# New TensorE prices in the list scheduler of a two-layer mixer and feed-forward kernel

## The chip, the cores and the metric

The kernel runs on one core of one Trainium2 chip. The metric is the device time of one execution in microseconds (us); the median of the runs is the figure to compare, and a profile of one execution says where the time goes.

The core has five engines that run at once, each through its own list of instructions in a fixed order: TensorE (PE in the profile; its weight loads are PEld), VectorE (DVE), ScalarE (ACT), GpSimd (POOL) and SyncE (SP), which here issues the DMA transfers. They wait for each other through semaphores.

## The reference

Two layers work on 256 latent tokens and 256 context tokens of width 1024. Each layer scales and shifts its input by values computed from a conditioning vector, runs four kinds of attention side by side, adds their projections through gates, projects the sum, normalises, and then runs a feed-forward network. The second layer computes the latent tokens alone.

```python
for l in range(DEPTH):                                   # DEPTH = 2
    mod_l = s_lat @ w_ada[l] + b_ada[l]                  # six rows of 1024: shifts, scales, gates
    hl = xl * (1.0 + sc1) + sh1                          # and the same for the context tokens
    out_l, out_c = token_mixers(hl, hc, ...)             # MLA, neighbourhood, differential, grouped-query
    xl = layer_norm(ALPHA * xl + g1 * out_l, ln1_g[l], ln1_b[l])
    hl = xl * (1.0 + sc2) + sh2
    xl = layer_norm(ALPHA * xl + g2 * swiglu(hl, w_gate_up[l], w_down[l]), ln2_g[l], ln2_b[l])
    # context tokens: the same, in the first layer only
```

In each attention, softmax(q k) over up to 512 keys multiplies v; the branch outputs are multiplied by sigmoid gates of the same input projection.

## The kernel before

Every float32 product is made of three matmuls on rounded operands: each operand is split into a high part (rounded to the type fp32r) and the rest, and high x high, high x low and low x high are summed (`mm3`). A weight block of 128 x 1024 is loaded by a DMA (tile `wr`), ScalarE rounds it (`wh`), and VectorE subtracts (`wl`). TensorE then runs over eight slices of 128 input channels with 512 moving columns (256 in the second layer). Softmax runs per head and per 128 queries: scores on TensorE (tile `st`), maximum on VectorE, exponential on ScalarE (tile `P`), scaling, then transposes of `P` on TensorE, a split of the result (`pth`, `ptl`), and the product with v (tile `o`).

The program doesn't emit these instructions as it meets them. `Plan.record` (line 249) notes each operation with the tiles that it reads and writes, and asks `price` (line 280) for its duration. When the whole program has been noted, `schedule` (line 313) orders it. It runs up to ten passes (PASSES, line 227). A pass has two halves:

- `forward` (line 382) plays the program through with the prices. Each engine is free again after the price of what it last ran. Among the operations of an engine that can start by then, the one of least priority number goes first. An operation can start when its predecessors have ended, plus an allowance for the signal between the two engines (SEE, lines 220 to 223), and when its tile has a buffer.
- `backward` (line 333) plays it from the end and gives each operation its priority for the next pass: how long before the end it has to run.

The pass whose modelled end is earliest is kept. `emit` (line 514) then writes the instructions out phase by phase, in the order of their modelled starts, so this sets the order of every engine's queue, the DMA queue of SyncE among them, and which buffer each tile takes. A new phase begins before the attention part of each layer and again before its feed-forward part. No modelled time reaches the chip: there only the order within each queue and the semaphores count.

The prices of the other engines stand in the same function: VectorE's is 0.065 us and one element a cycle at 0.96 GHz, ScalarE's 0.05 or 0.09 us and 0.833 ns an element, and a DMA's goes by its bytes.

All instructions are issued in `emit`, so the profile gives all of them line 535, and they are told apart by the names of their tiles.

Of the kernel before, what the change touches and what calls it, by code (L numbers as in the profile page):

```python
# [11 lines left out]
F32R = mybir.dt.float32r  # L12
# [219 lines left out]
class Plan:  # L232
# [47 lines left out]
    def price(self, op, ins, outs):  # L280

        eng, kw = op.eng, op.kw
        if eng == "tensor":
            if op.meth == "transpose":
                n = kw["in_"].shape[0]
                return max(64, n) * 2.1 / 2400
            n = max(64, kw["rhs"].free())
            return n / 2400 + 0.0026 if kw["rhs"].dtype == F32R else n * 4 / 2400 + 0.43
        n = max([v.free() for v in outs + ins] or [1])
        ps_in = any(v.tile.pool.psum for v in ins)  # L290
        ps = ps_in or any(v.tile.pool.psum for v in outs)
        if eng == "scalar":
            ptr = sum(1 for k in ("bias", "scale") if isinstance(kw.get(k), View)) + ("accum_out" in kw)
            return (0.05 if ps_in else 0.09) + n * 0.833e-3 + 0.093 * ptr
        if eng == "vector":
            if op.meth == "reciprocal":
                return 0.065 + n * 8 / 960
            ptr = sum(1 for k in ("scalar", "scalar1", "scalar2") if isinstance(kw.get(k), View))
            if op.meth == "tensor_scalar" or op.meth == "tensor_copy":
                return 0.065 + 0.06 * ptr + n / 960 / (1 if ps else 2)  # L300
            return 0.065 + 0.065 * ptr + n / 960
        if eng == "gpsimd":
            if kw.get("op") == ALU.pow:
                return 0.3 + n * 0.17
            return 0.16 + n * 2.2e-3
        op_bytes = 1
        for v in (outs or ins):
            op_bytes = v.shape[0] * v.free() * 4
        op.bytes = op_bytes
        op.dge = 0.65 if outs and ins else 0.46  # L310
        return 0.05
# [1513 lines left out]
```

## Time and profile before

| | before |
|---|---|
| median of 3 runs | 1371.51 us (1370.48 to 1372.27) |
| the profiled execution, its own time | 1370.68 us |
| its span, first to last instruction | 1368.9 us |
| TensorE busy | 1349.6 us, 99% |
| VectorE busy | 1007.4 us, 74% |
| ScalarE busy | 658.8 us, 48% |
| moved by DMA | 223.83 MB, 164 GB/s in the mean |

An engine is busy while an instruction of it is shown. Consecutive matmuls overlap in the profile, because each is shown until its modelled end while the next has already begun; the rate of TensorE is therefore read from the distance of two starts, and not from the length of one instruction. The idle time that a row shows before an instruction, and the engine and tile that ended it, come from the semaphores.

### The profile page before, as it was taken

What the parts mean: (1) busy time and instruction counts of PE and PEld (TensorE: products, weight loads), DVE (VectorE), ACT (ScalarE), POOL (GpSimd) and SP (SyncE); (2) the same over time, 40 slices, a digit from 0 to 9 for tenths busy, and PEclk for the clock granted to TensorE, in tenths of its full rate; (3) what the DMA queues carried; (4) which work ended last, traced back from release to release, by engine and by line L of the source; (5) the groups of instructions that cost most, each with busy time, mean ns of one, the idle gap of its engine ahead of it and who ended that gap; (6) DMA issues with size and microseconds to landing.
All of it is one profiled execution on the core that took longest, in us unless ns stands there. A gap on an engine that the chain in (4) does not pass through costs nothing.

```text
span 1368.9 us, 20741 instructions
## 1 busy us (share of the span) xinstructions
PE 1349.6 (99%) x7804; PEld 1176.9 (86%) x7804; DVE 1007.4 (74%) x1786; ACT 658.8 (48%) x1177; POOL 65.2 (5%) x123
## 2 busy tenths in 40 slices
PE   7999999999999999999999999999999999999997
PEld 5789889888878889888888888899999999899986
DVE  6787799997885768777655463768879878855554
ACT  6666576634663413232223112457856575544430
POOL 0000100032000000000000000101000200000000
PEclk9999999999999999999999999999999999999999
DMA  8843434344336614556666664255344457655550
GB/s 313 271 126 113 134 112 130 102 154 151 104 112 214 228 39 147 183 193 193 195 205 197 209 194 148 76 176 162 101 135 149 141 195 270 197 186 185 188 181 31
DMA packets 72820, 223.83 MB, mean 164 GB/s; under 512 B 9697, under 2 KB 13969, under 8 KB 72721
## 3 DMA queue, kind: packets, MB, share of 16 engines
q1 hardware_dynamic: 72720, 222.52, 50.6%
q8 instruction: 61, 1.00, 0.3%
q14 instruction: 39, 0.31, 0.1%
HBM read 212.76 MB, written 1.07 MB: 156 GB/s over the span
## 4 chain that ended last, share of the span: by engine, by line
PE 94%; DVE 2%; POOL 1%; ACT 1%; DMA 1%; issue 1%; POOLq 0%; DVEq 0%; SPq 0%; ACTq 0%
PE mm L535 83%; PE st L535 8%; PE o L535 3%; DMA wr<-in_w_a 0%; POOL rms L535 0%; DVE wl L535 0%; ACT wh L535 0%; DVE x L535 0%; DVE ptl L535 0%; POOL rk L535 0%; DMA wr<-in_w_ada 0%; DVE raw L535 0%; ACT raw L535 0%; POOL lnr L535 0%; ACT pth L535 0%
## 5 line engine op out<-in xcount | busy, mean ns | idle before, releaser
L535 ACT CAST wh<-wr 128x1024 fp32r<-128x1024 f32 (+2 forms) x261 | 265.7, 1024 | 386.4 <-PE mm L535 312.8
L535 PE MATMUL mm<-hh,wh 128*128 128x512 f32 (+1 forms) x1248 | 423.4, 340 | 0.8 <-ACT wh L535 0.7
L535 PE MATMUL mm<-hl,wh 128*128 128x512 f32 (+1 forms) x1246 | 422.8, 339 | 0.0
L535 PE MATMUL mm<-hh,wl 128*128 128x512 f32 (+1 forms) x1248 | 422.2, 339 | 0.0
L535 DVE TENSOR_TENSOR wl<-wr,wh 128x1024 fp32r<-128x1024 f32 (+3 forms) x260 | 308.6, 1191 | 141.9 <-ACT wh L535 138.3
L535 PEld LDWEIGHTS mm<-hh,wh 128*128 128x128 f32 x1248 | 235.8, 189 | 25.9 <-ACT wh L535 1.4
L535 PEld LDWEIGHTS mm<-hh,wl 128*128 128x128 f32 x1248 | 235.6, 189 | 24.4
L535 PEld LDWEIGHTS mm<-hl,wh 128*128 128x128 f32 x1246 | 235.5, 189 | 23.0
L535 DVE CUSTOM_DVE_ANT_0 y<-wr,silbc 128x1024 bf16<-128x1024 f32 x80 | 96.6, 1222 | 48.8 <-DMA wr<-in_w_ada 48.7
L535 PE MATMUL mm<-wl,hh 128*128 128x256 f32 (+3 forms) x344 | 110.4, 321 | 0.0
L535 PE MATMUL mm<-wh,hh 128*128 128x256 f32 (+3 forms) x344 | 110.2, 322 | 0.0
L535 PE MATMUL mm<-wh,hl 128*128 128x256 f32 (+3 forms) x344 | 110.2, 321 | 0.0
L535 PE MATMUL mm<-wl,fh 128*128 128x512 f32 (+1 forms) x270 | 101.6, 376 | 0.0
L535 PE MATMUL mm<-wh,fl 128*128 128x512 f32 (+1 forms) x270 | 101.6, 376 | 0.0
L535 PE MATMUL mm<-wh,fh 128*128 128x512 f32 (+1 forms) x270 | 101.4, 377 | 0.0
L535 DVE TENSOR_REDUCE s<-st 128x1 f32<-128x512 f32 (+1 forms) x120 | 70.7, 597 | 7.9 <-PE st L535 6.3
L535 ACT ACTIVATE P<-st,s 128x512 f32<-128x512 f32 (+1 forms) x96 | 59.0, 617 | 28.3 <-DVE s L535 27.6
L535 PE MATMUL mm<-y,wh 128*128 128x512 f32 (+1 forms) x256 | 68.7, 344 | 0.2 <-ACT wh L535 0.2
L535 PEld LDWEIGHTS mm<-wh,hh 128*128 128x128 f32 x344 | 64.7, 189 | 4.5 <-DVE y L535 0.3
L535 PEld LDWEIGHTS mm<-wh,hl 128*128 128x128 f32 x344 | 64.9, 189 | 4.0
L535 PEld LDWEIGHTS mm<-wl,hh 128*128 128x128 f32 x344 | 64.9, 189 | 3.7
L535 DVE TENSOR_TENSOR ptl<-st,pth 128x512 fp32r<-128x512 f32 (+1 forms) x96 | 56.4, 594 | 7.6 <-ACT pth L535 6.9
(273 smaller groups left out, 2021.3 us busy)
## 6 DMA issues: line engine op xcount, KB each, us to landing
wr<-in_w_ada SPq DMA_DIRECT2D x87, 512.0 KB, 3.7
wr<-in_w_gu SPq DMA_DIRECT2D x80, 512.0 KB, 4.3
wr<-in_wa SPq DMA_DIRECT2D x74, 512.0 KB, 3.7
wr<-in_w_dn SPq DMA_DIRECT2D x44, 512.0 KB, 3.4
wr<-in_w_br SPq DMA_DIRECT2D x16, 512.0 KB, 3.5
wr<-in_w_out SPq DMA_DIRECT2D x16, 512.0 KB, 5.4
wr<-in_w_gq SPq DMA_DIRECT2D x8, 512.0 KB, 3.4
bc<-in_lnrows SPq DMA_DIRECT2D x16, 256.0 KB, 3.3
```

Of the source, the lines that this page charges most:

```text
L535: o.ins = getattr(getattr(nc, o.eng), o.meth)(*args, **kw)
```

## The change

`price` gets new numbers for TensorE, and nothing else is edited. A transpose was priced by its rows at 2.1 cycles each; it now costs 0.108 us, or 0.09 us where its input has at most 32 rows. A matmul was priced by its columns at 2.4 GHz and 0.0026 us more (another formula stood for plain float32 operands); it now costs its columns, at least 256, at 2.4 GHz and 0.0134 us more.

```diff
         if eng == "tensor":
             if op.meth == "transpose":
-                n = kw["in_"].shape[0]
-                return max(64, n) * 2.1 / 2400
-            n = max(64, kw["rhs"].free())
-            return n / 2400 + 0.0026 if kw["rhs"].dtype == F32R else n * 4 / 2400 + 0.43
+                return 0.108 if kw["in_"].shape[0] > 32 else 0.09
+            return max(256, kw["rhs"].free()) / 2400 + 0.0134
```

The instructions, their operands and their phases stay the same. What may differ is their order in each engine's queue within a phase, and the buffer that a tile takes.

## Rows read from the trace of the kernel before

**Rows 1.** The page, part 1: busy us (share of the span) xinstructions, by engine.
```profile
PE 1349.6 (99%) x7804; PEld 1176.9 (86%) x7804; DVE 1007.4 (74%) x1786; ACT 658.8 (48%) x1177; POOL 65.2 (5%) x123
```

**Rows 2.** Busy time by stage: stretch, length, engines' busy us, granted clock, DMA share, GB/s.
```profile
0.00:40.00 40.00, 32.02 (x173) 20.89 (x174) 27.17 (x61) 26.83 (x41) 2.81 (x11) 1.00 0.90 319
...
400.00:410.00 10.00, 8.60 (x40) 6.62 (x39) 6.03 (x9) 6.97 (x9) 0.00 (x0) 1.00 0.05 14
...
515.00:868.00 353.00, 353.00 (x1619) 292.78 (x1618) 219.16 (x317) 90.87 (x116) 1.46 (x4) 1.00 0.57 181
...
1115.00:1125.00 10.00, 9.15 (x69) 8.13 (x68) 7.90 (x13) 5.94 (x9) 0.00 (x0) 1.00 0.26 82
...
1200.00:1360.00 160.00, 160.00 (x1162) 151.60 (x1161) 85.81 (x104) 63.69 (x88) 1.68 (x2) 1.00 0.48 154
1360.00:1369.00 9.00, 0.91 (x8) 0.70 (x6) 4.55 (x9) 0.00 (x0) 1.68 (x2) 0.78 0.31 117
sum 1369.00, PE 1349.62 PEld 1176.90 DVE 1007.38 ACT 658.76 POOL 65.21; mean PE 134.96 PEld 117.69 DVE 100.74 ACT 65.88 POOL 6.52
```

**Rows 3.** What TensorE's matmuls waited for: us in total, times, longest us.
```profile
PE st L535 <- ACT pth L535: 6.0, 1, 6.0
PE mm L535 <- DVE wl L535: 1.4, 1, 1.4
...
PE mm L535 <- ACT wh L535: 0.8, 3, 0.4
PE mm L535 <- ACT raw L535: 0.6, 1, 0.6
...
PE mm L535 <- DVE qr L535: 0.2, 1, 0.2
```

**Rows 4.** TensorE's timeline in three stretches: start us, length us, instruction (merged rows xcount).
```profile
700.18 0.39 PE L535 MATMUL mm<-hl,wh 128*128 128x512 f32 x1
700.41 0.39 PE L535 MATMUL mm<-hh,wl 128*128 128x512 f32 x1
...
1220.14 0.28 PE L535 MATMUL mm<-hh,wh 128*128 128x256 f32 x1
1220.26 0.28 PE L535 MATMUL mm<-hl,wh 128*128 128x256 f32 x1
...
201.62 0.60 PE L535 MATMUL st<-ident,P 128*128 128x128 f32 x4
201.98 0.48 PE L535 MATMUL mm<-hh,wh 128*128 128x512 f32 x1
202.29 0.40 PE L535 MATMUL mm<-hl,wh 128*128 128x512 f32 x1
```

**Rows 5.** TensorE's timeline at the end of the first attention part.
```profile
407.26 0.27 PE L535 MATMUL st<-ident,ada 128*8 128x128 f32 x1
408.94 0.50 PE L535 MATMUL mm<-y,wl 128*128 128x512 f32 x1 [1.40 <-DVE wl L535]
```

**Rows 6.** VectorE's timeline in an attention stage: a weight split and the next instruction.
```profile
229.52 1.23 DVE L535 TENSOR_TENSOR wl<-wr,wh 128x1024 fp32r<-128x1024 f32 x1
230.67 0.21 DVE L535 SCALAR_TENSOR_TENSOR s<-s,lam,dfs 128x1 f32<-128x1 f32 x1
```

**Rows 7.** TensorE's timeline in the second layer: a chain's last score matmul and its transposes.
```profile
970.34 0.39 PE L535 MATMUL st<-k,q 96*128 96x512 f32 x1
...
973.73 0.60 PE L535 MATMUL st<-ident,P 128*128 128x128 f32 x4
```

**Rows 8.** ScalarE's timeline there: the scaling of that chain's probabilities.
```profile
972.73 0.73 ACT L535 ACTIVATE P<-P,s 128x512 f32<-128x512 f32 x1
```

**Rows 9.** Instructions on tile P, whole span: the last step of every chain, by engine.
```profile
L535 ACT ACTIVATE P<-P,s x48: 710/724/739, 78.2 to 1111.5; 128x512 f32<-128x512 f32 x48
L535 DVE TENSOR_SCALAR P<-P,s x24: 332/354/357, 80.6 to 390.4; 128x256 f32<-128x256 f32 x24
L535 DVE SCALAR_TENSOR_TENSOR P<-P,s,P x24: 469/740/753, 225.8 to 1055.2; 128x512 f32<-128x512 f32 x16, 128x256 f32<-128x256 f32 x8
```

## The prediction

> **What bounds the kernel now.** I read the page's busy shares first, then the busy time by stage, then the list of what TensorE waited for, and last TensorE's own timeline. The page says TensorE: it is busy 1349.6 us of a span of 1368.9 us, VectorE 74% of it [rows 1]. The table by stage says where the rest is [rows 2]: its sum row has 1349.62 us busy in 1369.00 us, 19.38 us idle. The first 40 us hold 7.98 us of it and the last 9 us 8.09 us. That leaves 3.31 us for everything between 40 and 1360 us, of which 1.40 us lie at 400 to 410 us and 0.85 us at 1115 to 1125 us, where the attention part of a layer ends and its feed-forward part begins. The two long feed-forward stretches, 515 to 868 us and 1200 to 1360 us, hold none: 513 us in which no order can win idle time back. The list of waits [rows 3] has 6.0 us for the first weights in the head and six waits in the middle, of 1.4, 0.8 (three), 0.6 and 0.2 us. Not one of them is for the probabilities of a softmax chain.
>
> A caution on "busy": a matmul of 512 columns is shown as 0.39 us long while the next one starts 0.23 us behind it [rows 4], so idle time is shown only beyond the 0.16 us by which they overlap. The wait shown as 1.40 us is a gap from 407.26 to 408.94 us behind a transpose that takes 0.11 us: 1.57 us lost [rows 5]. For six such waits I add 6 x 0.16 = 1.0 us, so the stalls in the middle cost about 4.3 us.
>
> **The change part by part.** It changes numbers that only the planner reads. Each engine still gets the same instructions, on the same tiles' shapes, in the same phases; what may move is the order on every one of the five queues inside a phase, the DMA queue of SyncE included, and which buffer a tile gets.
>
> First, are the new prices what the trace shows? Matmuls of 512 columns start at 700.18 and 700.41 us, 0.23 us apart; those of 256 columns at 1220.14 and 1220.26 us, 0.12 us apart [rows 4]. The new price gives 512 / 2400 + 0.0134 = 0.2267 us and 256 / 2400 + 0.0134 = 0.1201 us; the old one gave 0.2159 and 0.1093 us. Four transposes and the matmul behind them take from 201.62 to 202.29 us; 0.67 us less 0.23 us for the matmul leaves 0.11 us for each transpose [rows 4], against 0.108 us new and 0.112 us old. So the new prices are right to about 3% and the old ones were 5% to 9% low on every matmul. The branch for plain float32 operands that goes had no user: every matmul here moves fp32r. It costs nothing.
>
> Second, what does that do to the plan's balance? The program issues 3630 matmuls of 512 columns, 3244 of 256, 198 of 384, 192 of 288 and 540 transposes, 7804 in all, as the page counts them [rows 1]. By the old prices they come to 1253.6 us, by the new ones to 1330.5 us: 7264 matmuls x 10.8 ns = +78.5 us, 524 transposes x -4 ns and 16 small ones x +34 ns = -1.6 us. Against 1349.6 us shown busy, the new sum leaves 19.1 us, or 2.4 ns an instruction, for overlap, small waits and switches between transposes and matmuls. The planner's VectorE prices already are intervals: a weight split of 1024 columns is priced at 0.065 + 1024 / 960 = 1.13 us, and the next instruction starts 1.15 us after it, though it is shown as 1.23 us long [rows 6]. So the old plan let TensorE run 6% too fast beside a VectorE priced rightly, and the new one has both right. TensorE stays the engine with the most work in either plan, so neither has a reason to leave it waiting on purpose.
>
> Third, the terms of the sum, against the profiled execution (span 1368.9 us, its run 1370.68 us, which is 0.83 us under the median of 1371.51 us; I carry the differences over to the median):
> - TensorE's work: 0. No instruction is added or removed. The granted clock is 1.00 in every stage but the last, that is at the 2.4 GHz level, and no gap here is big enough for me to expect a change [rows 2]. The 2.4 ns an instruction depend a little on the order (how often a transpose sits between matmuls); I let them stay and give them 2 us either way.
> - Head: 0. The first 6.0 us wait for the first weight block and its rounding, before any matmul can start [rows 3]; the DMA engines are 0.90 busy for 40 us [rows 2], so no order of matmuls makes the data come sooner. What could move is 7.98 - 6.0 = 2.0 us. If the order there got worse, that would cost about as much.
> - Feed-forward stretches: 0, with no idle time to win, and with VectorE at 219 us of 353 us and 86 us of 160 us as cover [rows 2]. If that cover went, a weight split that came late would cost one of its 1.15 us.
> - Tail: 0. Behind the last matmul runs a chain of VectorE, GpSimd and an output transfer that has no alternative order of consequence; 8.09 us stay.
> - The stalls in the middle, 4.3 us: all redrawn, since the planner tries ten passes, keeps the one whose modelled length is least, and now models another length. No row of before shows what the new order stalls on. Bounds: all gone, -4.3 us; or as many again, +4.3 us. With a truer TensorE the planner sees better when it will run out of matmuls at the two phase ends, so I take -1 us, half of their 2.25 us of shown idle time.
> - The softmax chains: 0 now, see the second rival; bounds 0 and +4.8 us. I take 0, as the tightest chain that I read still has its margin.
>
> Sum: -1 us, 1371.5 - 1.0 = 1370.5 us. What a measurement of this kernel can tell from no change is about 0.2%, 2.7 us, so the likeliest case is "no change".
>
> The Trainium skill speaks against the new prices: "TensorE: Matmul & The Clock Gate", section "Back-to-back issue gap", gives the warm gap of an isolated matmul as columns / 2.4 GHz plus about 2.5 ns, which is nearly the old price and would make TensorE's work here 1253.6 us. The trace disagrees, with 0.23 us for 512 and 0.12 us for 256 columns [rows 4] where that formula gives 0.216 and 0.109 us; by that formula the span would hold some 115 us of idle time, and it shows 19.4 us.
>
> **The rivals.**
> Faster: the old plan's error caused the stalls that are left, and with the right ratio they go. For it: the largest one, 1.40 us, is a wait for a VectorE weight split at a phase end [rows 2, 3], the kind that a planner with a wrong ratio misplaces. Against it: there is little to win. At most 4.3 us in the middle and 2.0 us in the head, 6.3 us; I take two thirds, -4.2 us: 1367.3 us.
>
> Slower: the old error was a safety margin, and the new plan spends it. Where the planner fills the time of a softmax chain with other matmuls, the old prices made it put in 5% to 9% more of them than fit. A chain from 970.34 us, its last score matmul, to 973.73 us, its first transpose, lasts 3.39 us [rows 7]; 4.8% of it (all 512 columns) is 0.16 us, 9% (all 256) 0.30 us. The scaled probabilities were done at 972.73 + 0.73 = 973.46 us [rows 8], so this chain had 0.27 us to spare: less 0.16 to 0.30 us, it sits about at zero, part of which the signal between engines takes. There are 48 + 24 + 24 = 96 such chains [rows 9]. For it: TensorE waits for none of them now [rows 3]. Against it: the planner has its own allowance for the signal between engines, and a chain is late only where nothing else is queued ahead of it. It decides from the point at which about a sixth of the chains (18 x 0.15 us = 2.7 us) come late; if a third do, by 0.15 us each, it is 32 x 0.15 = +4.8 us: 1376.3 us.
>
> The change does not do what it says: TensorE's stretches are so long beside the others' that the order where it matters stays as it is, and the time with it, 1371.5 us. For it: in the feed-forward stretches one engine sets the pace in either plan. Against it: a chain of 3.39 us holds over a dozen matmuls, so the prices move what fits into it by more than one of them. I count it within "no change".
>
> **How the numbers follow.** Forecast, no change beyond 2.7 us: 0.42. Faster rival: 0.33. Slower rival: 0.25. The range takes in the larger part of both rivals with the 2 us of the order's small costs: -6 us and +5.5 us around 1371.5 us, 1365.5 to 1377.0 us. For the likeliest case alone it is 1368.8 to 1374.2 us. Chances of faster by over 0.2%, within it and slower by over it: 0.33, 0.42, 0.25.
>
> **What would show it.** In the changed kernel's profile: 7804 TensorE instructions, the spacing of 0.23 and 0.12 us as before, and no idle time in the two long feed-forward stretches; if these change, my account of the work is wrong. The stalls of 1.40 and 0.85 us at the phase ends smaller: the forecast's step. TensorE waits on the probabilities or their splits in the attention stages, several of 0.1 to 0.2 us: the slower rival. I am wrong altogether if the head or the tail moves by more than 2 us, or if a new stall of several us stands at a phase end, which no row of before prices.

## The result: 1.6% slower, by stalls between the matmuls

The changed kernel takes 1393.13 us in the median of four runs (1391.85 to 1393.98), beside 1371.34 us for the kernel before on the same chip: a ratio of 1.0157 with a 95% interval of 1.0145 to 1.0169, or 21.8 us more. That is over four times the price that I gave to the slower rival, and above my range. The profiled execution took 1393.98 us with a span of 1392.2 us, 23.3 us above the span of before.

Line 1 of the page after, busy us by engine, answers to [rows 1]:

```profile
PE 1359.5 (98%) x7804; PEld 1176.9 (85%) x7804; DVE 1006.8 (72%) x1786; ACT 657.0 (47%) x1177; POOL 67.4 (5%) x123
```

The count of instructions is the same on every engine. VectorE and ScalarE are busy for as long as before, to 2 us. So no work was added. Here is the spacing of the matmuls in the feed-forward parts of both layers, TensorE's timeline of after (start us, length us, instruction), to be held against [rows 4]:

```profile
699.63 0.39 PE L533 MATMUL mm<-hl,wh 128*128 128x512 f32 x1
699.86 0.39 PE L533 MATMUL mm<-hh,wl 128*128 128x512 f32 x1
...
1219.73 0.28 PE L533 MATMUL mm<-hh,wh 128*128 128x256 f32 x1
1219.85 0.28 PE L533 MATMUL mm<-hl,wh 128*128 128x256 f32 x1
```

It is 0.23 and 0.12 us, as before: the new prices describe these streams as well after as before. Where the time went stands in the table of busy time by stage of after (stretch, length, busy us of PE, PEld, DVE, ACT and POOL, granted clock, DMA share, GB/s), which answers to [rows 2]:

```profile
0.00:40.00 40.00, 31.84 (x181) 21.07 (x182) 30.30 (x65) 28.60 (x44) 2.82 (x11) 1.00 0.93 331
40.00:400.00 360.00, 352.33 (x1938) 298.96 (x1936) 300.74 (x646) 211.59 (x457) 30.46 (x50) 0.99 0.42 128
...
410.00:515.00 105.00, 103.66 (x459) 83.56 (x458) 69.00 (x100) 40.41 (x55) 2.87 (x6) 1.00 0.47 157
515.00:868.00 353.00, 353.00 (x1645) 293.76 (x1644) 223.03 (x321) 93.41 (x120) 0.74 (x2) 1.00 0.58 182
868.00:1115.00 247.00, 241.66 (x1689) 224.10 (x1688) 194.44 (x386) 148.71 (x295) 24.26 (x46) 1.00 0.43 134
...
1125.00:1200.00 75.00, 72.87 (x484) 65.62 (x483) 62.02 (x100) 42.98 (x72) 2.85 (x4) 1.00 0.64 223
1200.00:1360.00 160.00, 160.00 (x1134) 150.12 (x1133) 94.09 (x114) 75.85 (x106) 0.00 (x0) 1.00 0.57 181
1360.00:1393.00 33.00, 24.18 (x158) 21.86 (x156) 14.19 (x22) 2.10 (x2) 3.36 (x4) 0.91 0.09 32
sum 1393.00, PE 1359.54 PEld 1176.91 DVE 1006.78 ACT 657.01 POOL 67.36; mean PE 135.95 PEld 117.69 DVE 100.68 ACT 65.70 POOL 6.74
```

Idle time of TensorE, stretch length less busy time: head 8.16 us (7.98 before), the two long feed-forward stretches 0 (0 before), the end 8.82 us (8.09 before; the last window runs 0.8 us past the span of 1392.2 us, so the end itself is 8.0 us as before). Between them it is 7.67 + 1.34 + 5.34 + 2.13 = 16.5 us, where before had 3.31 us. The attention stages hold 13.0 us of it, and the work that is late for it stands in the last stretch, which has 158 matmuls where before had 8.

The other 9.9 us of the difference stand as longer busy time (1359.54 to 1349.62 us), since a stall begins inside the 0.16 us by which a matmul is shown beyond its follower's start. The distances between the starts of all matmuls show the whole of it. Measured against the new prices, 15 distances in before are too long by more than 0.16 us, 8.1 us together, and 39 in after, 25.5 us together: 17.4 us more. One stretch of after is left out of that; it has another cause and adds 3.0 us. Smaller lengthenings add 2.9 us. The sum, 23.3 us, is the difference of the two spans.

That one stretch is a lower clock. Behind a stall in which TensorE starts nothing for 3.06 us, the granted clock is 0.50, the 1.2 GHz level, for 6 us. Matmuls of 512 columns then start 0.43 us apart in place of 0.23 us (the same view as the table, then TensorE's timeline):

```profile
353.80:359.80 6.00, 5.98 (x15) 4.84 (x16) 3.01 (x10) 3.51 (x9) 0.00 (x0) 0.50 0.01 4
...
357.37 0.63 PE L533 MATMUL mm<-hh,wl 128*128 128x512 f32 x1
357.80 0.63 PE L533 MATMUL mm<-hh,wh 128*128 128x512 f32 x1
```

What the stalls wait for is in the list of TensorE's waits of after (us in total, times, longest), against [rows 3]:

```profile
PE st L533 <- ACT pth L533: 6.0, 1, 6.0
PE st L533 <- DMA q<-raw: 4.3, 2, 2.7
PE mm L533 <- DVE qr L533: 2.6, 4, 0.9
PE st L533 <- DVE ptl L533: 1.9, 3, 0.9
PE mm L533 <- ACT wh L533: 1.9, 5, 0.5
PE mm L533 <- DVE wl L533: 1.4, 3, 0.5
...
PE st L533 <- ACT P L533: 0.8, 1, 0.8
```

The first row is the head, as before, and so are 1.6 us of the `ptl` row, which fall into the first 14 us. From 40 us on the shown waits come to 16.1 us. Two kinds stand out. Scores (`st`) wait 4.3 us for `q<-raw`, a copy from SBUF to SBUF that puts one half of a tile into another's partitions; before had no such wait. Matmuls that transpose `qr` wait 2.6 us (0.2 us before), and `qr` itself is held up by GpSimd. Together these are 6.9 of the 16.1 us. The steps of the softmax chains, which my slower rival named, hold 2.1 us of it, weight blocks (`wh` and `wl`) 3.3 us, and the rest is spread over many tiles.

**The copies.** SyncE's timeline of after (SPq: issue times) and, in the second fence, TensorE's:

```profile
344.58 0.33 SPq L533 DMA_DIRECT2D wr<-in_w_br  x1
346.36 0.33 SPq L533 DMA_DIRECT2D wr<-in_wa  x1
347.26 0.50 SPq L533 DMA_DIRECT2D k<-k  x1
347.81 1.53 SPq L533 DMA_DIRECT2D q<-raw  x2
```

```profile
350.76 0.39 PE L533 MATMUL mm<-hl,wh 128*128 128x512 f32 x1
353.82 0.76 PE L533 MATMUL st<-k,q 128*128 128x512 f32 x1 [2.67 <-DMA q<-raw]
```

The copies go out 2.7 and 0.9 us behind two weight loads of 512 KB. Three us after the last matmul the scores start. The rows of the DMA issues (engine op xcount, KB each, median us to landing) give after first, before second:

```profile
k<-k SPq DMA_DIRECT2D x12, 128.0 KB, 5.0
q<-raw SPq DMA_DIRECT2D x8, 128.0 KB, 3.9
```

```profile
k<-k SPq DMA_DIRECT2D x12, 128.0 KB, 2.4
q<-raw SPq DMA_DIRECT2D x8, 128.0 KB, 2.4
```

The medians go by the copies whose landing the trace shows; for `q<-raw` these are five in after and two in before. The planner models all transfers as one queue that moves so many bytes a microsecond, and lets a tile be used 0.95 us after the modelled end of its transfer.

**GpSimd.** The timeline of after around one of the waits for `qr` (all engines, other lines left out):

```profile
302.06 1.21 DVE L533 CUSTOM_DVE_ANT_0 raw<-wr,silbc 128x1024 bf16<-128x1024 f32 x1
302.19 1.18 POOL L533 TENSOR_SCALAR rms<-rms 128x4 f32<-128x4 f32 x1
...
304.74 0.23 POOL L533 TENSOR_SCALAR rms<-rms 128x4 f32<-128x4 f32 x1
304.86 1.22 DVE L533 TENSOR_TENSOR wl<-wr,wh 128x1024 fp32r<-128x1024 f32 x1
305.05 1.92 POOL L533 TENSOR_TENSOR rms<-rms,mhalf 128x4 f32<-128x4 f32 x1
307.00 0.42 DVE L533 TENSOR_TENSOR qr<-st,rms 128x256 f32<-128x256 f32 x1 [0.93 <-POOL rms L533]
307.48 0.33 PE L533 MATMUL mm<-ident,qr 128*128 128x128 f32 x1 [0.90 <-DVE qr L533]
```

The same small instruction on 128 x 4 elements takes 0.23 us at 304.74 and 1.18 us at 302.19, where VectorE had begun an instruction 0.13 us earlier; it ends 0.1 us after that one does. The power at 305.05 takes 1.92 us beside a weight split, and VectorE (0.93 us) and TensorE (0.90 us) wait for it in turn. The planner prices the first kind at 0.17 us and the power on four columns at 0.3 + 4 x 0.17 = 0.98 us, whatever VectorE does.

So the theory after the result: these two delays, and others like them, are longer than the planner believes. With the old prices TensorE's stretches in the plan were 5% to 9% too short, so the planner put in more matmuls ahead of each wait, and this excess covered the delays. True prices took the cover away. The two kinds named are less than half of the shown waits, so the theory needs the others too. Rivals: (a) the softmax chains' signal allowances are what is short (my recorded rival); (b) the order is a draw, and any disturbance of the prices gives some other time; (c) the copies stand too long in SyncE's list.

### The profile page after: what moved, and what is told of

It is laid out like the page before. It is cut to its first block, busy times and chain, and to the rows that moved or that the text cites. A ratio compares the mean times of both kernels' runs of the same rounds, so it can differ in the third digit from the quotient of the medians.

```text
span 1392.2 us, 20749 instructions
## 1 busy us (share of the span) xinstructions
PE 1359.5 (98%) x7804; PEld 1176.9 (85%) x7804; DVE 1006.8 (72%) x1786; ACT 657.0 (47%) x1177; POOL 67.4 (5%) x123
## 4 chain that ended last, share of the span: by engine, by line
PE 85%; DVE 6%; ACT 3%; DMA 3%; POOL 1%; issue 1%; POOLq 0%; DVEq 0%; SPq 0%; ACTq 0%
PE mm L533 76%; PE st L533 7%; PE o L533 3%; DVE wl L533 1%; ACT wh L533 1%; POOL rms L533 1%; DVE s L533 1%; ACT P L533 1%; DMA q<-raw 1%; DVE x L533 1%; DVE ptl L533 1%; DMA wr<-in_w_ada 1%; DMA wr<-in_w_out 0%; POOL rk L533 0%; DMA wr<-in_wa 0%
## 5 line engine op out<-in xcount | busy, mean ns | idle before, releaser
L533 DVE CUSTOM_DVE_ANT_0 raw<-wr,silbc 128x1024 bf16<-128x1024 f32 x48 | 58.1, 1215 | 5.9 <-DMA wr<-in_w_ada 5.9
```

The lines of the kernel that those rows point to most:

```text
L533: o.ins = getattr(getattr(nc, o.eng), o.meth)(*args, **kw)
```

## The experiments

All times are medians; ratios are to the kernel before on the same chip, whose medians lay between 1371.13 and 1371.97 us. "Old" and "new" prices are TensorE's of before and of after.

### Which of the new numbers does it

`mm_only` and `tr_only` make one half of the change each, the matmuls (first diff) and the transposes (second).

```diff
-            n = max(64, kw["rhs"].free())
-            return n / 2400 + 0.0026 if kw["rhs"].dtype == F32R else n * 4 / 2400 + 0.43
+            return max(256, kw["rhs"].free()) / 2400 + 0.0134
```

```diff
-                n = kw["in_"].shape[0]
-                return max(64, n) * 2.1 / 2400
+                return 0.108 if kw["in_"].shape[0] > 32 else 0.09
```

> Only the matmul price changes, the transposes keep the old one (0.112 us). Margin theory: the old, too short matmul price made the planner put more matmuls into each wait than fit, and that hid waits which it prices too short; the matmul price carries that, so 1388 to 1398 us. Redraw theory (every price edit draws a new order, and the changed kernel got a bad one): anything from 1366 to 1395 us. If the transposes carry it: within 3 us of 1371 us.

> Only the transpose price changes (0.108 us, 0.09 us for the small ones), the matmuls keep the old one. Margin theory: the matmul price alone counts, 1369 to 1375 us. Redraw theory: anything from 1366 to 1395 us. If the transposes carry it: 1388 us or more.

Measured: `mm_only` 1393.78 us, 1.0167 [1.0152, 1.0182], the whole loss; `tr_only` 1382.35 us, 1.0080 [1.0065, 1.0095], half of it, from a change of 4 ns a transpose. The two don't add up, so one cause by parts is too simple. `tr_big` and `tr_small` divide the second:

```diff
-                return max(64, n) * 2.1 / 2400
+                return 0.108 if n > 32 else 64 * 2.1 / 2400
```

```diff
-                return max(64, n) * 2.1 / 2400
+                return 0.09 if n <= 32 else n * 2.1 / 2400
```

> Old prices, but the 524 large transposes at 0.108 us in place of 0.112; the small ones keep 0.056. If they carry the loss: 1379 to 1386 us. If not: 1369 to 1374 us. Margin theory alone has no place for a loss from 4 ns; redraw theory has.

> Old prices, but the 16 small transposes at 0.09 us in place of 0.056. If the head's order sets what follows, 1380 us or more; if the 524 large ones do it, 1369 to 1374 us.

`tr_small` 1370.67 us, 0.9997 [0.9988, 1.0006]: nothing. `tr_big` 1382.21 us, 1.0077 [1.0062, 1.0092]: the 524 large transposes do it, 0.112 to 0.108 us each. Its list of TensorE's waits:

```profile
PE st L535 <- DMA q<-raw: 2.3, 1, 2.3
...
PE mm L535 <- DVE qr L535: 2.0, 1, 2.0
```

The copies and `qr` stand here too, beside others of the same size. The edit takes 524 x 4 ns = 2.1 us off the work that the planner sees, and the time is 11 us longer: it shifts which instructions meet, and the margin alone can't say why.

### Is it the luck of the draw, and does it grow with the price

`jit_before_a`, `jit_before_b` and `jit_after_a` scatter TensorE's prices by up to 1% from one operation to the next, with the mean kept (`_b` has 59 for 37).

```diff
+            if op.eng == "tensor":
+                op.cost *= 1 + 0.01 * ((op.idx * 37 % 101) / 50 - 1)
```

> The old prices, each TensorE price multiplied by a factor between 0.99 and 1.01 that follows the operation's number and is 1 in the mean: a new order without a change of the balance. Margin theory: 1368 to 1376 us, near the kernel before. Redraw theory: as far off as the changed kernel is, 10 to 25 us.

> The new prices with the same factors between 0.99 and 1.01. Margin theory: 1386 to 1398 us, near the changed kernel. Redraw theory: the changed kernel was a bad draw, so another draw falls back by 10 us or more, 1366 to 1383 us.

> The old prices with a second set of factors between 0.99 and 1.01, 1 in the mean. If the old prices give a good order as a rule: 1368 to 1376 us. If the kernel before is a rare draw: 1378 us or more.

Old prices: 1372.86 us, 1.0011 [1.0001, 1.0021], and 1370.43 us, 0.9988 [0.9978, 0.9997]. New prices: 1390.44 us, 1.0140 [1.0125, 1.0155]. Such a draw moves either kernel by 1.5 to 2.7 us, and the 21.8 us between them stay. So neither kernel is a rare draw among orders at its own prices, and rival (b) falls as an account of the whole. But the scatter is small, 2.3 ns at most on a matmul of 512 columns. It doesn't bound what a shift of all prices does: 4 ns on the transposes alone gave 11 us. A difference of about 10 us between single runs below can therefore still be such a jump.

The waits of `jit_after_a` are other ones than after's. The two kinds named have 1.3 and 1.8 us, and its longest is 3.2 us for the rounding of a weight block. The loss at the new prices isn't tied to the copies and GpSimd alone.

`dose_8` and `dose_m8` put the matmul's constant between old and new (0.0026 and 0.0134 us), and as far below the old one, with old transposes.

```diff
+            return kw["rhs"].free() / 2400 + 0.0080
```

```diff
+            return kw["rhs"].free() / 2400 - 0.0082
```

> Matmul price halfway: columns / 2.4 GHz + 0.0080 us, old transposes. Margin theory: between the two, 1373 to 1386 us. Redraw theory: no order in the size, anything from 1366 to 1395 us.

> The matmul price as far under the old one as the new one is above it (columns / 2.4 GHz - 0.0082 us), old transposes. Margin theory: more margin than before does not hurt the chains, but the plan runs out of matmuls for other waits: 1366 to 1378 us, and fewer waits on GpSimd and on the copies than the changed kernel. Redraw theory: anything up to 1395 us.

`dose_8` 1380.06 us, 1.0063 [1.0046, 1.0080]: half the dose, 40% of the loss. `dose_m8` 1383.02 us, 1.0086 [1.0071, 1.0101]: a still cheaper TensorE, which by the margin alone should lose nothing, loses 11.9 us. Its longest waits behind the head are others than after's:

```profile
PE mm L534 <- DVE wl L534: 3.2, 4, 1.4
PE mm L534 <- ACT raw L534: 3.0, 3, 2.3
```

VectorE's weight splits and ScalarE's results come first; the copies have 1.0 us. A TensorE that is too cheap in the plan seems to run out of matmuls there in the plan as well, and the planner accepts it; that part is argued, and a jump of the order as in `tr_big` is as large. What follows is that, of the prices tried, the old one is the best and both sides are slower, so the time isn't a point on one slope.

### Which delays were covered

These keep the new prices and lengthen one allowance each, in the order of the diffs: `m_see` the signal from ScalarE and VectorE to TensorE, `m_dma` the time from a transfer's end to its use, `m_pool` GpSimd's instructions. `m_both` is the first two, `m_pool_dma` the last two, `m_all` the last two with half the first.

```diff
-SEE = {"tensor": {"tensor": 0.0}, "scalar": {"scalar": 0.1, "tensor": 0.24, "gpsimd": 0.07},
-       "vector": {"vector": 0.128, "tensor": 0.23, "gpsimd": 0.156}, "gpsimd": {"gpsimd": 0.1, "vector": 0.07},
+SEE = {"tensor": {"tensor": 0.0}, "scalar": {"scalar": 0.1, "tensor": 0.44, "gpsimd": 0.07},
+       "vector": {"vector": 0.128, "tensor": 0.43, "gpsimd": 0.156}, "gpsimd": {"gpsimd": 0.1, "vector": 0.07},
```

```diff
-                dma = max(dma, t + 0.95) + max(op.bytes / 360e3, op.dge)
-                free[e] = dma - 0.95
+                dma = max(dma, t + 1.95) + max(op.bytes / 360e3, op.dge)
+                free[e] = dma - 1.95
...
-                op.end = dma_free + 0.95
+                op.end = dma_free + 1.95
```

```diff
-                return 0.3 + n * 0.17
-            return 0.16 + n * 2.2e-3
+                return 0.6 + n * 0.25
+            return 0.4 + n * 2.2e-3
```

> The new prices, and 0.2 us more in the planner's allowance for a signal from ScalarE or VectorE to TensorE (0.24 to 0.44 and 0.23 to 0.43 us). Margin theory: the waits on other engines go, those on transfers stay: 1378 to 1389 us. Redraw theory: no direction, 1366 to 1395 us.

> The new prices, and 1.0 us more in the planner's time from a transfer's end to its use (0.95 to 1.95 us). Margin theory: the waits on moved q and k tiles and on late weight blocks go, those on softmax chains stay: 1372 to 1385 us. Redraw theory: no direction, 1366 to 1395 us.

> The new prices with both allowances raised, 0.2 us for signals to TensorE and 1.0 us for transfers. Margin theory: the margin is given back where it belongs, so at or below the kernel before, 1360 to 1372 us. Redraw theory: no direction, 1366 to 1395 us.

> The new TensorE prices, and GpSimd's prices raised to what its short operations take (0.16 to 0.40 us; powers from 0.3 + 0.17 us a column to 0.6 + 0.25). Margin theory, with GpSimd's price as one of those too short: the stalls of transposes behind a power (qr and raw, about 4.4 us) go, the rest stays: 1384 to 1390 us. Redraw theory: no direction, 1366 to 1395 us.

> The new TensorE prices, GpSimd's prices raised as before and 1.0 us more from a transfer's end to its use. Margin theory: both kinds of stall shrink, 1366 to 1378 us. Redraw theory: near the same plan without GpSimd's part, 1380 to 1385 us.

> The new TensorE prices with GpSimd's prices raised, 1.0 us more for transfers and 0.1 us more for signals from ScalarE and VectorE to TensorE. Margin theory: the waits on probabilities and splits that are left (about 2.4 us) go as well, 1370 to 1376 us. Redraw theory: 1372 to 1384 us.

| kernel | us (range) | ratio [95%] | of the 21.8 us back |
|---|---|---|---|
| m_see | 1394.52 (1393.06 to 1396.84) | 1.0168 [1.0153, 1.0183] | none |
| m_dma | 1382.88 (1380.99 to 1384.08) | 1.0080 [1.0065, 1.0095] | 10.3 |
| m_both | 1383.08 (1381.09 to 1386.06) | 1.0085 [1.0070, 1.0100] | 10.1 |
| m_pool | 1383.82 (1381.62 to 1384.98) | 1.0090 [1.0075, 1.0105] | 9.3 |
| m_pool_dma | 1376.95 (1375.84 to 1377.26) | 1.0040 [1.0026, 1.0055] | 16.2 |
| m_all | 1380.50 (1379.91 to 1380.80) | 1.0059 [1.0044, 1.0074] | 12.6 |

The last column is 1393.13 less the median. Longer signals bring nothing, alone or on top of the others. In `m_both` no wait for a step of a softmax chain is left behind the head, and the time is that of `m_dma`: rival (a) falls. The waits of `m_pool_dma` show what is left with the two others; `q<-raw` and `qr` are gone from the list:

```profile
PE st L533 <- ACT pth L533: 6.1, 1, 6.1
PE mm L533 <- ACT raw L533: 1.5, 2, 1.3
PE st L533 <- ACT P L533: 1.4, 3, 0.8
PE mm L533 <- DVE wl L533: 1.3, 2, 1.0
```

The single edits are less clean. In `m_dma` the waits are these, so its 10.3 us did not come from the one wait that it was meant for:

```profile
PE st L533 <- DMA q<-raw: 3.4, 2, 2.1
PE mm L533 <- DVE qr L533: 3.0, 4, 1.0
```

In `m_pool`, which leaves the transfers' price alone, both kinds are gone as well, with 1.2 us for the other copy in their place, and only 9.3 us come back:

```profile
PE mm L533 <- ACT wh L533: 2.9, 5, 1.4
...
PE st L533 <- DMA k<-k: 1.2, 1, 1.2
```

So neither allowance acts on its own wait alone; that of `m_dma` also holds for every weight load. I take only the pair as shown: with both, the two kinds of wait vanish and three quarters of the loss comes back, 16.2 us, more than any jump seen here. That it comes back because these two waits vanish isn't shown, and how much belongs to each can't be read from runs whose order jumps by up to 11 us.

`mv_act` tests (c). It keeps after's order, but ScalarE's queue issues the copies.

```diff
+        self.nc.ops[-1].lab = "move"
...
+                            eng = "scalar" if getattr(o, "lab", None) == "move" else o.eng
```

> The order of the changed kernel, unaltered; only the transfers inside SBUF that copy q and k halves (tiles q from raw, k from k) are issued by ScalarE instead of SyncE. If these waits come from standing behind weight loads in SyncE's list, the score matmuls' stalls (7.1 us in ten, 4.3 us of it shown as waits on those transfers) fall under 3 us and the time to 1385 to 1390 us. If the copies themselves are slow, or ScalarE holds them back, the stalls stay: 1390 to 1398 us.

Measured: 1393.94 us, 1.0165 [1.0149, 1.0180], no change against after. The first copy of the group goes out 0.9 us behind the same weight load as in after, so it hadn't stood in SyncE's list. The copies land no sooner (DMA issues), and the scores still wait 2.43 us (TensorE's timeline):

```profile
k<-k ACTq DMA_DIRECT2D x12, 128.0 KB, 5.9
q<-raw ACTq DMA_DIRECT2D x8, 128.0 KB, 4.7
```

```profile
353.35 0.94 PE L534 MATMUL st<-k,q 128*128 128x512 f32 x3 [2.43 <-DMA q<-raw]
```

Rival (c) falls: the delay is behind the issue, in the transfers. The Trainium skill has a rule for this, in "DMA: Bandwidth & Descriptors", section "Issuing engines are not separate DMA queues": transfers started by different engines run on the same 16 DMA engines and interleave there. This run agrees, 4.7 us from ScalarE's queue beside 3.9 us from SyncE's.

### What the old price is worth once the delays are in the plan

Both allowances of `m_pool_dma` with the old prices (`b_pool_dma`), and with a matmul halfway and new transposes (`m_half_pd`); the edits of `m_dma` and `m_pool` stand in both.

```diff
-            return max(256, kw["rhs"].free()) / 2400 + 0.0134
+            return max(256, kw["rhs"].free()) / 2400 + 0.0080
```

> The old TensorE prices with GpSimd's prices raised and 1.0 us more from a transfer's end to its use. If the old matmul price only stands in for these allowances, it is worth nothing beside them: 1372 to 1380 us, like the new prices with the same allowances (1376.95 us). If it gives margin of its own: under 1370 us.

> GpSimd's prices raised, 1.0 us more for transfers, and the matmul price halfway (columns / 2.4 GHz + 0.0080 us). Margin theory: what is left of the loss, waits on ScalarE and VectorE of 0.3 to 1.5 us, shrinks by this smaller margin: 1366 to 1374 us. Redraw theory: 1370 to 1384 us without direction.

`b_pool_dma` 1374.41 us, 1.0020 [1.0011, 1.0029]; `m_half_pd` 1374.85 us, 1.0031 [1.0019, 1.0042]; `m_pool_dma`, with the new ones, 1376.95 us. Without the allowances old and new prices lie 21.8 us apart, with them 2.5 us, which is the size of a redraw. That is the strongest evidence for the cover: three kernels with these two allowances alone and different prices of TensorE lie together, most of what the old price bought the allowances buy as well, and beside them it is worth next to nothing. It speaks for plans that leave more room; it doesn't name the waits that needed it. In `b_pool_dma` the copies land as late as in after, and yet no wait for them is in TensorE's list:

```profile
k<-k SPq DMA_DIRECT2D x12, 128.0 KB, 4.3
q<-raw SPq DMA_DIRECT2D x8, 128.0 KB, 5.1
```

So a late copy costs nothing where the plan has put other matmuls ahead of its user. Not every range held. The margin theory's failed for `tr_only`, `dose_m8`, `m_see`, `m_both` and `m_all`, and by under 1 us for `m_pool` and `m_half_pd`. Those of the redraw theory were mostly too wide to fail; they failed for the three scattered kernels and `m_pool_dma`. No kernel of the study is faster than before by more than a redraw: the best, `jit_before_b`, is 1.5 us below it on its chip.

## Why the prediction was wrong, step by step

- The prices against the trace: right. The spacing is 0.23 and 0.12 us in after as well. The Trainium skill's gap of columns / 2.4 GHz plus about 2.5 ns, which "TensorE: Matmul & The Clock Gate", section "Back-to-back issue gap", gives for an isolated matmul, is not the spacing in these streams in either trace, as the prediction said.
- TensorE's work, the feed-forward stretches, the head and the tail at 0: right. 7804 instructions, no idle time in 513 us, the head within 0.2 us and the end unchanged at 8.0 us.
- The granted clock, from whose stage rows the prediction expected no change: right for before, wrong for the new order. A gap of 3.06 us between two starts stands ahead of 6 us at the 1.2 GHz level, which cost 3.0 us in the profiled execution.
- "The old plan let TensorE run 6% too fast beside a VectorE priced rightly, and the new one has both right": here the reasoning broke. I checked the price of one VectorE instruction and spoke as if every other engine were right. GpSimd and the copies, which I never priced, were short: 1.92 us for a power priced at 0.98 us, and 3.9 and 5.0 us to landing for copies that took 2.4 us before. TensorE's price was short as well, and one error made up for the others in part, as the kernels with `m_pool_dma`'s allowances tell.
- The stalls in the middle, bounded by -4.3 and +4.3 us: this is the term that failed. Shown idle time there went from 3.3 to 16.5 us, and with its hidden parts and the lower clock the whole term is about +22 us. "As many again" was no bound: the stalls that before shows are those that were left under the cover, and say nothing of those that the cover hid. What would have bounded it is the delays themselves: copies of 2.4 us to landing that a weight load ahead can stretch, 20 of 128 KB in the trace, and GpSimd instructions whose longest time is five times their median.
- The slower rival, "the old error was a safety margin": right in kind, wrong in place and size. I priced the softmax chains at 4.8 us. In after, from 40 us on, `ptl`, `P` and the products behind them wait 2.1 us, under half of that, and 14.0 of the 16.1 us of waits lie elsewhere: behind copies, GpSimd, weight blocks and others. Its remedy, a longer signal (`m_see`), brought nothing.
- The faster rival and "the change does nothing": both wrong. The stall of 1.40 us behind a weight split went, as the faster rival wanted (the longest wait for `wl` in after is 0.5 us), and over 20 us of others came.
- "I am wrong altogether if a new stall of several us stands at a phase end": it came, of 2.67 us, within the attention stage and not at its end. I named the event and gave it no price.

Open: why 4 ns on the large transposes turn the order into one that is 11 us worse, and with it how much of the 21.8 us is cover and how much the order that these prices happen to give; how the 10.3 and 9.3 us of the two allowances divide among single waits; and the 5.6 us by which `m_pool_dma` still lies above the before of the first comparison, for which a longer signal gave no cause, and a lower price of TensorE at most 2.5 us. A planner that prices a GpSimd instruction by what VectorE does at that moment, or a copy by the loads in flight, wasn't tried. Which of its passes the planner keeps doesn't part slow from fast: played through from the kernels' own source, it is the second in after and the ninth in `jit_after_a`, the fourth in before and the third in `tr_small`.

## What to carry to other kernels

A price in a list scheduler that is known to be too low may be making up for another that is too low as well: before correcting one, compare every engine's prices, and the landing times of small transfers, with their longest time in the trace and not their median. Bound the cost of a new order by the delays that exist in the kernel (how late each can be, times how often), and not by the stalls that the present order happens to show. Where a change only redraws an order, scatter the prices by 1% first: the spread is the least by which single orders differ. It is no upper bound; here it was 1.5 to 2.7 us, and a shift of 4 ns on one kind of instruction gave 11 us.

## What the runs showed of the hardware

A GpSimd instruction can last until a VectorE instruction that began before it has ended. One kind of instruction on tile `rms` on GpSimd, whole span of after (ns min/median/max):

```profile
L533 POOL TENSOR_SCALAR rms<-rms x12: 222/224/1177, 279.9 to 1079.0; 128x4 f32<-128x4 f32 x12
```

Of the 52 TENSOR_SCALAR instructions that GpSimd runs in after, 39 take 0.19 to 0.25 us. The other 13 take 0.48 to 1.18 us, and each of them began while VectorE was in an instruction with two operands in SBUF (a weight split, `raw<-wr,silbc`, `x<-x,bc`) and ended 0.05 to 0.1 us after it; beside VectorE instructions that read PSUM (`raw<-mm,l`) they take 0.19 us. The Trainium skill has this, in "SBUF — State Buffer", section "SBUF: two separate sides": GpSimd and a VectorE instruction with two SBUF inputs hold a common port in turn, each for its whole length. The traces agree; no run took VectorE's instruction away to show it as a cause.

Copies of 128 KB from SBUF to SBUF land later close behind weight loads. In before the `k<-k` copy at 343.71 us, 4.4 us behind the last load of 512 KB, lands 2.4 us after its issue, and the one at 1082.02 us, 0.55 us behind a load, 4.1 us after it. In after the two `q<-raw` copies at 348.88 and 350.16 us, behind loads at 344.58 and 346.36 us, take 5.4 and 4.7 us. No run moved the loads away to show them as the cause.
